# Moving operands read word by word from two places in turn

## The chip, the core and the metric

The kernel runs on one core of one Trainium2 chip. The metric is the device time of one execution, in microseconds; lower is better. Before the change the median of three runs is 2076.68 us (2076.17 to 2077.5). The engines are called by the names in the profile: PE is TensorE's matmuls and PEld its weight loads, DVE is VectorE, ACT ScalarE, POOL GpSimd, SP SyncE.

A matmul holds one operand, the weights or *stationary* operand (128 x 128), in the array. The other, the *moving* operand, is read from the on-chip memory word by word, one column of 128 partitions after the other, and the results go to PSUM in the same order.

## What is computed

One decoder layer on 512 tokens of width 2048, float32: two groups of attention heads side by side, then a gated feed-forward.

```python
def reference(x, attn_norm, w_in, ..., w_out, ffn_norm, w_gate, w_up, w_down):
    h = _rms_norm(x, attn_norm)
    proj = h @ w_in                   # 8 FoX heads (q, k, v, forget gates), 8 NSA heads (q), 2 KV groups x 6, gates
    # FoX: q, k normed per head; softmax(q k' * scale + cum_f[query] - cum_f[key]), causal
    # NSA: compressed keys and values (32-token blocks, stride 16), selected blocks, sliding window,
    #      each a softmax with a distance penalty, added under sigmoid gates
    x = x + concat(o_fox, o_nsa) @ w_out
    h = _rms_norm(x, ffn_norm)
    x = x + (silu(h @ w_gate) * (h @ w_up)) @ w_down     # 5632 wide
    return x
```

## The kernel before

Activations lie transposed: 128 features on the partitions, tokens along the free dimension. Every float32 operand is split into a high part that the matmul's rounded format holds exactly and the low rest, and each product is three matmuls: high x high, high x low, low x high (`mm3`, L258). ScalarE makes the high part and VectorE the low part by subtraction (`split`, L194; `split2`, L208; most of their instructions stand under L92 and L95, the helpers `tt` and `act`).

The stages, in order of time:

- **First loop** (L881): for 16 blocks of input features, load x and four columns of weights, split both, and accumulate the inputs of the compression (`first`, 512 columns, L259 to L261). `scaled` (L389) takes them out of PSUM; for these four results it writes them regrouped for the compression, at a step of 32 words (L394).
- **Projections** (`gemm_steps`, L293; `proj`, L399): 16 heads in 48 matmuls of 512 columns each, with the normalized activations `xg` (in `bigm`) as the moving operand. `values` (L500) makes pairs of value heads the other way round: the activations are stationary, and the weights, 256 columns, move (L540). With `gcols` (the first pair) it also makes the gates. `normed` and `query` turn the results into keys and queries. They run interleaved with the attention heads (`nsa`, L815; `fox`, L839) by hand-written generators (`weave`, `stagger`).
- **Compression** (`compress`, L698): 32 small products per kind, the weights moving.
- **Seven products** (`seven`, L1039): for the last head pairs, a 2 x 2 block product is made with seven products of half size. The forms of the activations (`form`, L1007) move, 256 columns (L1057), and the results are combined from PSUM into two tiles (L1059 to L1079).
- **Output projection**: heads `oT` are split into `om` (`om_parts`, L1201); some column blocks go directly (`two_tiles`, `one_tile`, 512 columns), six by seven products (`one_of_seven`, L1366, 256 columns; sums of heads from `activation_sums`, L1208). `x1_steps` adds the residual, and `raw_forms` (L1242) puts the next stage's inputs, scaled, into four quarters of a raw tile; `form_sums` and `form_parts` make the seven forms from them.
- **Gate and up** (L1763 to L1814): 22 column blocks x gate and up x 4 groups = 176 groups of 42 matmuls with 256 columns (L1792). For each group, SP loads four weight blocks (`fetch`), VectorE makes three sums of them (`sums`), ScalarE the high parts and VectorE the low parts (`part_steps`, L1609), into two slots of `bigm` by turns. A slot can be written again when the matmuls two groups earlier are done. Results of a block are combined on VectorE (`put_together`, `gate_out`, `up_out`) while the next one is computed, in a second set of PSUM banks.
- **Down** (L1888 to L1961): four passes over 22 blocks; each block loads its activations (`load_a`, from DRAM) and weights, splits both (`splits`, L1716), and runs 48 or 36 matmuls of 256 columns (L1931 high weights, L1936 low weights).

From the output projection on, VectorE and ScalarE keep the program's order (`pinned`); in the last two stages the loads do too. All weights are reordered on the host in `kernel`, before the launch.

Of the kernel before, what the change touches and what calls it, by code (L numbers as in the profile page):

```python
# [83 lines left out]
def hybrid_layer(ctx: ExitStack, tc: tile.TileContext, xT, vec, ffb, wfg, wfirst, win, cmpw, wout, wos, wgu, wdn, out):  # L84
# [172 lines left out]

    def mm3(o, lh, ll, rh, rl, start, stop):  # L258
        nc.tensor.matmul(o, lh, rh, start=start, stop=False)  # L259
        nc.tensor.matmul(o, lh, rl, start=False, stop=False)  # L260
        nc.tensor.matmul(o, ll, rh, start=False, stop=stop)  # L261
# [31 lines left out]
    def gemm_steps(o, srcs, mov, name):  # L293

        k = 0
        for j, src in enumerate(srcs):
            wp = load_w(src, f"{name}_{j}")
            for kk in range(src.shape[-1] // P):
                s = slice(kk * P, (kk + 1) * P)
                mm3(o, wp[0][:, s], wp[1][:, s], mov[k][:, 0, :], mov[k][:, 1, :],  # L300
                    k == 0, k == len(mov) - 1)
                k += 1
                yield
# [85 lines left out]
    def scaled(z, name, early=False):  # L389
        t = oxp.tile([P, T], F32, tag="ox", name=f"t_{name}", bufs=OXB) if early else ftile(f"t_{name}")  # L390
        if early:

            b, c = [x.rearrange("p (n l) -> p n l", l=16) for x in (z, rstd)]
            nc.vector.tensor_tensor(t.rearrange("p (l n) -> p n l", l=16), b, c, op=OP.mult)  # L394
        else:
            nc.vector.tensor_tensor(t, z, rstd, op=OP.mult)
# [17 lines left out]
    def squares(name, z):  # L414
# [3 lines left out]
        nc.scalar.activation(sq[half], z[half], AF.Square)  # L418
        nc.scalar.activation(sb[half], z[second_half], AF.Square)
# [34 lines left out]
    def query(name, gain):  # L454
# [3 lines left out]
        split2(r, z, gain)  # L458
        sq = squares(name, z)
# [40 lines left out]
    def values(pair, gcols=None):  # L500
# [10 lines left out]
        for c in range(4):  # L511
# [22 lines left out]
            for b in range(2):  # L534
                for kk in range(4):
                    x = xg[4 * c + kk]
                    for t in range(2):
                        at = slice((2 * b + t) * P, (2 * b + t + 1) * P)
                        for n, xp in enumerate((0, 0, 1)):
                            nc.tensor.matmul(z[2 * b + t][:, :cols[n]], x[:, xp, at], wp[n][kk],  # L540
                                             start=(c == 0 and kk == 0 and n == 0 and (t == 0 or gcols is not None)),
                                             stop=(c == 3 and kk == 3 and n == 2), skip_group_check=True)
# [155 lines left out]
    def compress(which):  # L698
# [3 lines left out]
        for b in range(8):  # L702
# [4 lines left out]
            for jj in range(4):  # L707
                l = 4 * b + jj
                ws = slice(jj * P, (jj + 1) * P)
                nc.tensor.matmul(z, live[which, l // 16][:, l % 16 * P:(l % 16 + 1) * P], wp[:, :, ws],  # L710
                                 start=(l == 0), stop=(l == 31))
# [169 lines left out]
    for k in range(NK):  # L881
# [15 lines left out]
        if k == 0:  # L897
            for wi, xi in ((0, 0), (1, 0), (0, 1)):
                for j in range(4):
                    nc.tensor.matmul(first[j], wp[:, wi, j * P:(j + 1) * P], t[:, xi], start=(wi + xi == 0), stop=False)  # L900
        else:
            for j in range(4):
                c = slice(j * P, (j + 1) * P)
                mm3(first[j], wp[:, 0, c], wp[:, 1, c], t[:, 0], t[:, 1], False, k == NK - 1)
# [134 lines left out]
    def seven(key, names):  # L1039
# [5 lines left out]
        for step, (to, f) in enumerate(products(n)):  # L1045
# [8 lines left out]
            for m, (wp, u, xp) in enumerate(todo):  # L1054
                if m and m % 6 == 0:
                    yield
                nc.tensor.matmul(z, w[wp][:, u * P:(u + 1) * P], form(f, u)[xp], start=(fresh and m == 0),  # L1057
                                 stop=(m == len(todo) - 1), skip_group_check=True)
            if f == 0:  # L1059
                nc.scalar.activation(t0[:, upper], z, AF.Copy)  # L1060
            elif f == 5:
                nc.vector.tensor_tensor(t1[:, lower], z, t0[:, upper], op=OP.add)
            elif f == 4:
                nc.vector.tensor_tensor(t1[:, upper], z, t1[:, upper if n else lower], op=OP.subtract)
            elif f == 1:
                nc.vector.tensor_tensor(t0[:, lower], z, rstd[:, lower], op=OP.mult)
            elif f == 3 and to == 1:
                nc.vector.tensor_tensor(t1[:, upper], z, t0[:, upper], op=OP.add)
            elif f == 6:
                nc.vector.tensor_tensor(t1[:, lower], z, t1[:, lower], op=OP.subtract)  # L1070
            elif f == 2:
                nc.vector.tensor_tensor(t0[:, upper], z, t0[:, upper], op=OP.add)
            else:
                nc.vector.tensor_tensor(t1[:, upper], t1[:, upper], z, op=OP.subtract)
                nc.vector.tensor_tensor(t0[:, upper], z, t0[:, upper], op=OP.add)
# [125 lines left out]
    def om_parts(i):  # L1201
        split(om[i], oT[order[i]])
# [5 lines left out]
    def activation_sums():  # L1208

        last = None  # L1210
        for u in range(HALF):
# [6 lines left out]
            for i in range(2):  # L1218
# [6 lines left out]
                dst = [osums_a[:, u, p, 2 * i:2 * i + 2] for p in range(2)]  # L1225
                act(dst[0], f[i], AF.Copy)
                if last:
                    tt(last[0][1], last[1], last[0][0].bitcast(F32), op=OP.subtract)
                last = dst, f[i]
# [817 lines left out]
```

## Time and profile before

| what | us |
|---|---|
| median of three runs | 2076.68 |
| profiled execution, span | 2076.6 |
| PE busy | 2058.7 |
| PEld busy | 1974.0 |
| DVE busy | 1802.1 |
| ACT busy | 1070.6 |
| POOL busy | 322.5 |
| gate and up, first matmul to first of down (812.14 to 1652.65) | 840.5 |

The profiled execution takes as long as the runs do. "Busy" is the time in which at least one instruction of the engine ran. Matmuls overlap one another in the pipeline, so a busy TensorE says only that there was always a matmul in flight; how fast they follow each other is the time of a stretch over the number that ran in it. Rows of groups have the form: line, engine, operation, output tile <- input tiles, shapes, count | busy us, mean ns of one | idle time before them and what ended it.

### The profile page before, as it was taken

Reading aid. Unit: us, or ns where it says so; the run is one execution under the profiler, and the core shown is the slowest. Engines: PE = TensorE matmul, PEld = TensorE weight load, DVE = VectorE, ACT = ScalarE, POOL = GpSimd, SP = SyncE. Lnnn points to the kernel's source line nnn. Section 1 sums busy time; section 2 is a strip of 40 time slices with the busy share of each in tenths; the row PEclk is TensorE's granted clock in tenths of the full one; section 3 lists DMA queues with packets and bytes.
Section 4 is the critical chain, followed back from the end, with each engine's and each line's share of the span. In section 5 each row is a group of like instructions: output and inputs, shape, how many; then the busy total and the mean of one; then the engine's idle time right before and its main releaser. Section 6 shows DMA issues by size and latency. Waiting matters only on the chain.

```text
span 2076.6 us, 40008 instructions
## 1 busy us (share of the span) xinstructions
PE 2058.7 (99%) x16189; PEld 1974.0 (95%) x16189; DVE 1802.1 (87%) x2744; ACT 1070.6 (52%) x1408; POOL 322.5 (16%) x489
## 2 busy tenths in 40 slices
PE   9999999999999999999999999999999999999999
PEld 7878988899998988999999999999999999999999
DVE  6678779887787877999999999999999987889998
ACT  6555555567675555443343434433433455565554
POOL 1032232422121011111111111111111000000010
PEclk9999999999999999999999999999999999999999
DMA  5685776967785675667767777777777897579865
GB/s 207 205 184 163 179 177 175 221 188 203 223 208 174 203 231 183 176 197 183 201 186 197 195 182 204 190 184 200 186 190 199 254 325 251 153 240 331 295 179 149
DMA packets 142153, 424.22 MB, mean 204 GB/s; under 512 B 17608, under 2 KB 17608, under 8 KB 141968
## 3 DMA queue, kind: packets, MB, share of 16 engines
q1 hardware_dynamic: 91168, 289.21, 41.4%
q0 software_dynamic: 44176, 106.19, 26.7%
q10 hardware_dynamic: 6624, 26.27, 3.3%
q8 instruction: 126, 2.06, 0.4%
q14 instruction: 59, 0.48, 0.1%
HBM read 389.34 MB, written 124.53 MB: 247 GB/s over the span
## 4 chain that ended last, share of the span: by engine, by line
PE 82%; issue 8%; DVE 6%; ACT 2%; POOL 2%; DMA 1%; POOLq 0%; ACTq 0%; SPq 0%; DVEq 0%
PE q L1792 40%; PE pd L1931 13%; PE pd L1936 7%; PE ps_vs L540 2%; PE po L1381 2%; PE ps_vf L540 2%; PE ps_qn L259 1%; PE ps_qn L261 1%; PE ps_qn L260 1%; PE ps_first L261 1%; POOL osum L141 1%; PE ps_first L259 1%; PE po L261 1%; PE po L259 1%; PE po L260 1%
## 5 line engine op out<-in xcount | busy, mean ns | idle before, releaser
L95 ACT ACTIVATE bigm<-r 128x1792 fp32r<-128x1792 f32 x174 | 298.3, 1714 | 467.1 <-PE q L1792 290.9
L92 DVE TENSOR_TENSOR bigm<-r,bigm 128x1792 fp32r<-128x1792 f32 x174 | 351.5, 2020 | 13.2 <-ACT bigm L95 12.5
L92 DVE TENSOR_TENSOR r<-r 128x512 f32<-128x512 f32 x522 | 267.2, 512 | 26.1 <-DMA r<-wgu 13.9
L141 POOL DMA_DIRECT2D wsum<-wdn x176 | 120.3, 690 | 702.3 <-ACT bigm L95 609.6
L1792 PE MATMUL q<-bigm 128*128 128x256 f32 x1848 | 217.4, 276 | 0.5 <-ACT bigm L95 0.3
L1792 PE MATMUL q<-formy,bigm 128*128 128x256 f32 x1848 | 217.0, 276 | 0.0
L1792 PE MATMUL q<-forma,bigm 128*128 128x256 f32 x1848 | 216.8, 276 | 0.0
L1792 PE MATMUL q<-formx,bigm 128*128 128x256 f32 x1848 | 216.8, 276 | 0.0
L1792 PEld LDWEIGHTS q<-bigm 128*128 128x128 f32 x1848 | 213.2, 188 | 0.9 <-ACT bigm L95 0.5
L1792 PEld LDWEIGHTS q<-formy,bigm 128*128 128x128 f32 x1848 | 212.9, 188 | 0.2
L1792 PEld LDWEIGHTS q<-forma,bigm 128*128 128x128 f32 x1848 | 213.0, 188 | 0.1
L1792 PEld LDWEIGHTS q<-formx,bigm 128*128 128x128 f32 x1848 | 212.9, 188 | 0.0
L1931 PE MATMUL pd<-bigm 128*128 128x256 f32 x1200 | 146.9, 276 | 0.0
L1931 PEld LDWEIGHTS pd<-bigm 128*128 128x128 f32 x1200 | 141.0, 188 | 0.0
L92 DVE TENSOR_TENSOR bigm<-wd,bigm 128x1024 fp32r<-128x1024 f32 (+1 forms) x62 | 107.8, 1739 | 12.4 <-ACT bigm L95 12.2
L95 ACT ACTIVATE bigm<-rawm 128x768 fp32r<-128x768 f32 (+2 forms) x72 | 66.0, 927 | 97.8 <-PE pd L1936 63.2
L95 ACT ACTIVATE bigm<-wd 128x1024 fp32r<-128x1024 f32 (+1 forms) x62 | 91.1, 1470 | 10.7 <-DVE wd L92 6.1
L92 DVE TENSOR_TENSOR bigm<-rawm,bigm 128x768 fp32r<-128x768 f32 (+2 forms) x72 | 75.6, 1059 | 23.2 <-ACT bigm L95 22.6
L1936 PE MATMUL pd<-bigm 128*128 128x256 f32 x600 | 80.7, 276 | 0.0
L141 POOL DMA_DIRECT2D fsump<-win x72 | 48.6, 743 | 204.2 <-ACT wp_qn L95 47.6
L1057 PE MATMUL ps_kf<-bigm,wp_kf 128*128 128x256 f32 x576 | 76.1, 281 | 0.7 <-ACT wp_kf L95 0.4
L1936 PEld LDWEIGHTS pd<-bigm 128*128 128x128 f32 x600 | 74.3, 188 | 0.0
(592 smaller groups left out, 4336.2 us busy)
## 6 DMA issues: line engine op xcount, KB each, us to landing
r<-wgu SPq DMA_DIRECT2D x174, 512.0 KB, 4.5
wsum<-wdn POOLq DMA_DIRECT2D x176, 256.0 KB, 5.1
rawm<-ad SPq DMA_DIRECT2D x44, 512.0 KB, 6.9
wd<-wdn SPq DMA_DIRECT2D x40, 512.0 KB, 6.1
wd<-wsum SPq DMA_DIRECT2D x40, 512.0 KB, 7.1
ad<-cb ACTq DMA_DIRECT2D x22, 896.0 KB, 6.6
fsump<-win POOLq DMA_DIRECT2D x72, 256.0 KB, 6.0
rawm<-ad SPq DMA_DIRECT2D x44, 384.0 KB, 3.5
```

Of the source, the lines that this page charges most:

```text
L92: return pin(nc.vector.tensor_tensor(*args, op=op))
L95: return pin(nc.scalar.activation(*args, **kw))
L141: d = nc.gpsimd.dma_start(step[0], step[1], **step[2])
L259: nc.tensor.matmul(o, lh, rh, start=start, stop=False)
L260: nc.tensor.matmul(o, lh, rl, start=False, stop=False)
L261: nc.tensor.matmul(o, ll, rh, start=False, stop=stop)
L540: nc.tensor.matmul(z[2 * b + t][:, :cols[n]], x[:, xp, at], wp[n][kk], start=(c == 0 and kk == 0 and n == 0 and (t == 0 or gcols is not No ...
L1057: nc.tensor.matmul(z, w[wp][:, u * P:(u + 1) * P], form(f, u)[xp], start=(fresh and m == 0), stop=(m == len(todo) - 1), skip_group_check=True)
L1381: nc.tensor.matmul(q[b][:, h * 256:(h + 1) * 256], w[wp][:, u * P:(u + 1) * P], a[xp], start=(h == 0 and u == 0 and wp == 0 and xp == 0), ...
L1792: nc.tensor.matmul(o, w[wp][:, fb, cs], a[:, xp, fa], start=(k == 0 and h == 0 and wp == 0 and xp == 0), stop=(g == NG - 1 and kk == 1 and ...
L1931: nc.tensor.matmul(b[q][k][:, h * 256:(h + 1) * 256], w[0][:, fb, q * P:(q + 1) * P], a[xp][:, fa], start=(j == 0 and h == 0 and xp == 0), ...
L1936: nc.tensor.matmul(b[q][k][:, h * 256:(h + 1) * 256], w[1][:, fb, q * P:(q + 1) * P], a[0][:, fa], start=False, stop=(j == NJ - 1), skip_g ...
```

## The change

Four views of a row of words are added. In the names below n is the row's length, cut into j equal pieces, and each piece into two halves.

- `_in_turn`: read word 0 of the first half, word 0 of the second, word 1 of the first, and so on.
- `_like`: the same shape over words as they lie (the output of a matmul that reads `_in_turn`).
- `_mixed`: every second word, first the even ones, then the odd ones.
- `_apart`: the two halves, one after the other; the same shape as `_mixed`.

```python
def mm(o, w, x, j=1, **kw):
    nc.tensor.matmul(_like(o, j), w, _in_turn(x, j), **kw)

def mm3t(o, lh, ll, rh, rl, start, stop, j=1):
    mm(o, lh, rh, j, start=start, stop=False)
    mm(o, lh, rl, j, start=False, stop=False)
    mm(o, ll, rh, j, start=False, stop=stop)

def _in_turn(x, j=1): return x.rearrange("p (j b a) -> p j a b", j=j, b=2)
def _like(x, j=1):    return x.rearrange("p (j a b) -> p j a b", j=j, b=2)
def _mixed(x, j=1):   return x.rearrange("p (j a b) -> p j b a", j=j, b=2)
def _apart(x, j=1):   return x.rearrange("p (j b a) -> p j b a", j=j, b=2)
```

The matmuls of `gemm_steps`, the first loop, `values` without `gcols`, `compress`, `seven`, the output projection, gate and up, and down use them; those of the attention, of the transposes and of `values` with `gcols` stay as they were. PSUM is written in order. So that results mean the same tokens, either the operand is written in a changed order or the result is read in one:

- Projections, first loop, `seven`: the activations lie as before, so the results lie mixed in PSUM. What takes them out reads `_mixed` and writes `_apart`:

```diff
-            nc.vector.tensor_tensor(t, z, rstd, op=OP.mult)
+            nc.vector.tensor_tensor(_apart(t), _mixed(z), _apart(rstd), op=OP.mult)
...
-        split2(r, z, gain)
-        sq = squares(name, z)
+        split2([_apart(x) for x in r], _mixed(z), gain)
+        sq = squares(name, z, _mixed)
...
-                nc.vector.tensor_tensor(t1[:, lower], z, t0[:, upper], op=OP.add)
+                nc.vector.tensor_tensor(l1, z, u0, op=OP.add)
```

  with `z = _mixed(z)` and `l0, u0, l1, u1` the `_apart` views of the two halves of `t0` and `t1`. The regrouping of the four first results (L394) reads a step of two as well.
- Output projection, gate and up, down: the parts are written `_apart` from a `_mixed` read, and the results lie in order:

```diff
-        split(om[i], oT[order[i]])
+        split2([_apart(om[i][:, p], 2) for p in range(2)], _mixed(oT[order[i]], 2))
...
-        act(raw[:, 1:3] if second else raw[:, 0:8:7], t.rearrange("p (h t) -> p h t", h=2), AF.Copy, scale=v1(V_FN + n))
+        for h, f in enumerate((1, 2) if second else (0, 7)):
+            act(_apart(raw[:, f]), _mixed(t[:, h * 256:(h + 1) * 256]), AF.Copy, scale=v1(V_FN + n))
...
-            split2(a, rawa.pop(i))
+            split2([_apart(x, n) for x in a], _mixed(rawa.pop(i), n))
```

  In `activation_sums` the same is done for the sums of heads.
- `values` and `compress`, where weights move: the host writes them in the changed order (`_unmix`, for the value pairs after the first and for `cmpw`).

The matmul of gate and up, as an example of all:

```diff
-                                nc.tensor.matmul(o, w[wp][:, fb, cs], a[:, xp, fa],
-                                                 start=(k == 0 and h == 0 and wp == 0 and xp == 0),
-                                                 stop=(g == NG - 1 and kk == 1 and wp == 1), skip_group_check=True)
+                                mm(o, w[wp][:, fb, cs], a[:, xp, fa],
+                                   start=(k == 0 and h == 0 and wp == 0 and xp == 0),
+                                   stop=(g == NG - 1 and kk == 1 and wp == 1), skip_group_check=True)
```

More of the change, by code (lines that the diff above doesn't have):

```diff
@@ L412, in hybrid_layer, with squares @@
     second_half = slice(P // 2, P)
-    def squares(name, z):
+    def squares(name, z, laid=_apart):
         sq = ftile(f"sq_{name}")
         sb = ap_.tile([P, T], F32, tag="sb", name=f"sb_{name}")
-        nc.scalar.activation(sq[half], z[half], AF.Square)
-        nc.scalar.activation(sb[half], z[second_half], AF.Square)
+        nc.scalar.activation(_apart(sq[half]), laid(z[half]), AF.Square)
+        nc.scalar.activation(_apart(sb[half]), laid(z[second_half]), AF.Square)
         nc.vector.tensor_tensor(sq[half], sq[half], sb[half], op=OP.add)
@@ L539, in values @@
                         for n, xp in enumerate((0, 0, 1)):
-                            nc.tensor.matmul(z[2 * b + t][:, :cols[n]], x[:, xp, at], wp[n][kk],
-                                             start=(c == 0 and kk == 0 and n == 0 and (t == 0 or gcols is not None)),
-                                             stop=(c == 3 and kk == 3 and n == 2), skip_group_check=True)
+                            (nc.tensor.matmul if gcols is not None else mm)(
+                                z[2 * b + t][:, :cols[n]], x[:, xp, at], wp[n][kk],
+                                start=(c == 0 and kk == 0 and n == 0 and (t == 0 or gcols is not None)),
+                                stop=(c == 3 and kk == 3 and n == 2), skip_group_check=True)
                     yield
@@ L709, in compress @@
                 ws = slice(jj * P, (jj + 1) * P)
-                nc.tensor.matmul(z, live[which, l // 16][:, l % 16 * P:(l % 16 + 1) * P], wp[:, :, ws],
-                                 start=(l == 0), stop=(l == 31))
+                nc.tensor.matmul(z.rearrange("p s (a b) -> p s a b", b=2), live[which, l // 16][:, l % 16 * P:(l % 16 + 1) * P],
+                                 wp[:, :, ws].rearrange("p s (b a) -> p s a b", b=2), start=(l == 0), stop=(l == 31))
                 if l % 2:
@@ L899, in hybrid_layer @@
                 for j in range(4):
-                    nc.tensor.matmul(first[j], wp[:, wi, j * P:(j + 1) * P], t[:, xi], start=(wi + xi == 0), stop=False)
+                    mm(first[j], wp[:, wi, j * P:(j + 1) * P], t[:, xi], start=(wi + xi == 0), stop=False)
         else:
@@ L1224, in activation_sums @@
                     tt(f[1][:, 1], f[1][:, 0], b[:, 0], op=OP.add)
-                dst = [osums_a[:, u, p, 2 * i:2 * i + 2] for p in range(2)]
-                act(dst[0], f[i], AF.Copy)
+                dst = [_apart(osums_a[:, u, p, 2 * i:2 * i + 2].rearrange("p f t -> p (f t)"), 2) for p in range(2)]
+                src = _mixed(f[i].rearrange("p f t -> p (f t)"), 2)
+                act(dst[0], src, AF.Copy)
                 if last:
                     tt(last[0][1], last[1], last[0][0].bitcast(F32), op=OP.subtract)
-                last = dst, f[i]
+                last = dst, src
                 yield
@@ L1380, in one_of_seven @@
                 for xp in range(2 - wp):
-                    nc.tensor.matmul(q[b][:, h * 256:(h + 1) * 256], w[wp][:, u * P:(u + 1) * P], a[xp],
-                                     start=(h == 0 and u == 0 and wp == 0 and xp == 0),
-                                     stop=(u == HALF - 1 and wp == 1), skip_group_check=True)
+                    mm(q[b][:, h * 256:(h + 1) * 256], w[wp][:, u * P:(u + 1) * P], a[xp],
+                       start=(h == 0 and u == 0 and wp == 0 and xp == 0),
+                       stop=(u == HALF - 1 and wp == 1), skip_group_check=True)
     loads, front, behind = {}, {}, {}
@@ L1742, in splits @@
         if i == 4 * NJ - 1:
-            split2(a, rawa.pop(i))
+            split2([_apart(x, n) for x in a], _mixed(rawa.pop(i), n))
         return [[x.rearrange("p (f c) -> p f c", f=n) for x in y] for y in (w, a)]
@@ L1930, in block @@
                                 for xp in range(2):
-                                    nc.tensor.matmul(b[q][k][:, h * 256:(h + 1) * 256], w[0][:, fb, q * P:(q + 1) * P], a[xp][:, fa],
-                                                     start=(j == 0 and h == 0 and xp == 0), stop=False, skip_group_check=True)
+                                    mm(b[q][k][:, h * 256:(h + 1) * 256], w[0][:, fb, q * P:(q + 1) * P], a[xp][:, fa],
+                                       start=(j == 0 and h == 0 and xp == 0), stop=False, skip_group_check=True)
                     for q in qs:
@@ L2030 @@
         "win": win,
-        "cmpw": np.concatenate(cw, axis=0),
+        "cmpw": _unmix(np.concatenate(cw, axis=0), P, np),
         "wout": _tiles(wo, np),
```

54 lines of the change are left out of this document (34 added, 20 removed).

## Prediction

> **What bounds the kernel now.** I read the page's first two parts and its shares of the chain that ended last, then the table by stretches, then single stretches of TensorE's timeline, and last who waits for whom.
>
> ```profile
> span 2076.6 us, 40008 instructions
> PE 2058.7 (99%) x16189; PEld 1974.0 (95%) x16189; DVE 1802.1 (87%) x2744; ACT 1070.6 (52%) x1408; POOL 322.5 (16%) x489
> ...
> PEclk9999999999999999999999999999999999999999
> ...
> PE 82%; issue 8%; DVE 6%; ACT 2%; POOL 2%; DMA 1%; POOLq 0%; ACTq 0%; SPq 0%; DVEq 0%
> ```
>
> TensorE is busy 99% of the span at its full granted clock and is 82% of the chain. So the question is whether its matmuls stream as fast as they could. The table by stretches (gate and up; down; output projection; everything from the first projections to the last heads) gives their pace:
>
> ```profile
> core 0: us, PE busy (x) PEld busy (x) DVE busy (x) ACT busy (x) POOL busy (x), PEclk, DMA share, GB/s
> 860.00:1640.00 780.00, 780.00 (x6882) 780.00 (x6881) 740.02 (x991) 313.93 (x225) 113.81 (x166) 1.00 0.74 193
> 1660.00:2060.00 400.00, 400.00 (x3528) 400.00 (x3527) 346.98 (x360) 228.11 (x230) 15.10 (x23) 1.00 0.76 246
> 670.00:810.00 140.00, 138.61 (x858) 123.65 (x857) 110.94 (x154) 75.78 (x90) 15.90 (x29) 1.00 0.63 207
> 100.00:670.00 570.00, 559.62 (x3709) 504.18 (x3708) 457.04 (x1013) 356.55 (x724) 159.59 (x235) 1.00 0.73 192
> ```
>
> In gate and up one matmul of 256 columns takes 780.00/6882 = 113.3 ns, in down 400.00/3528 = 113.4 ns, with no gap anywhere. The timeline of a stretch of the output projection has the 512-column ones; between the two rows lie 24 others:
>
> ```profile
> 654.26 0.40 PE L260 MATMUL po<-bigm,wp_o 128*128 128x512 f32 x1
> ...
> 659.94 0.39 PE L261 MATMUL po<-bigm,wp_o 128*128 128x512 f32 x1
> ```
>
> That is (659.94 - 654.26)/25 = 227.2 ns. The two widths fit one line through nothing: 113.3/256 = 0.443 ns a column, 227.2/512 = 0.444. There is no fixed cost per matmul in it, but a cost per word read. A matmul with few columns is bounded by its weight load instead; the timeline and the by-line view of the transposes:
>
> ```profile
> 249.80 0.60 PE L633 MATMUL pT_s<-ident,p_s 128*128 128x128 f32 x4
> L633 PE MATMUL pT_s<-ident,p_s x80: 270/272/329, 148.2 to 371.7; 128*128 128x128 f32 x80
> ```
>
> Four in 600 ns of which the last takes its whole 272: (600 - 272)/3 = 109 ns each, with 128 columns and a weight load each. So a new 128x128 weight every 109 ns is possible, and 113.3 ns for 256 columns isn't the weight load. It is the moving operand. As an estimate from these rows, a column could take 109/256 = 0.426 ns at most, if its word came in time; 0.443 is taken.
>
> The Trainium skill (TensorE: Matmul & The Clock Gate, Back-to-back issue gap) puts a warm matmul at N/2.4 + 2.5 ns, which is 109.2 and 215.8 ns here; the trace disagrees by 4.1 and 11.4 ns.
>
> Does the place of a read matter? In gate and up, group 55 of 176 has its low weight part 8 words further on (L1613, i % 48 == 7). Three rows of the timeline, one group each:
>
> ```profile
> 1071.62 4.92 PE L1792 MATMUL q<-formy,bigm 128*128 128x256 f32 x42
> 1076.38 5.02 PE L1792 MATMUL q<-bigm 128*128 128x256 f32 x42
> 1081.24 4.93 PE L1792 MATMUL q<-forma,bigm 128*128 128x256 f32 x42
> ```
>
> From its start to the next one's the first group takes 4.76 us, the second 4.86. The second differs in that shift (and in which form it reads), and 0.10 us over its 14 matmuls with low parts is 7 ns each. So the pace hangs on where words are read, and a new order of reading can move it.
>
> **The change part by part.** (1) **The matmuls.** The same instructions, columns and PSUM places; only the moving words come alternately from two places, 128 words apart (256 in the projections with 512 columns). Its count, by line (L1792, L1931, L1936, L1057, L1381 in this order, busy of each over the whole span):
>
> ```profile
> 0.00:2077.00 2077.00, 839.90 (x7392) 839.22 (x7392) 1.00 0.72 204
> 0.00:2077.00 2077.00, 297.37 (x2464) 287.58 (x2464) 1.00 0.72 204
> 0.00:2077.00 2077.00, 158.12 (x1232) 148.30 (x1232) 1.00 0.72 204
> 0.00:2077.00 2077.00, 169.86 (x1344) 162.55 (x1344) 1.00 0.72 204
> 0.00:2077.00 2077.00, 58.32 (x504) 57.91 (x504) 1.00 0.72 204
> ```
>
> and, from the by-line view, the value projections that change, and the first and last of the seven 512-column groups on L260:
>
> ```profile
> L540 PE MATMUL ps_vf<-wp_vf,bigm 128*128 128x256 f32 x384 | 53.0, 283 | 0.2 <-ACT sb_qf L419 0.2
> L540 PE MATMUL ps_vs<-wp_vs,bigm 128*128 128x256 f32 x192 | 27.5, 284 | 0.0
> ...
> L260 PE MATMUL po<-bigm,wp_o 128*128 128x512 f32 x160 | 62.5, 391 | 0.0
> ...
> L260 PE MATMUL ps_ks<-bigm,wp_ks 128*128 128x512 f32 x32 | 12.5, 391 | 0.0
> ```
>
> Gate and up have 7392, down 2464 + 1232 = 3696, the rest 1344 + 504 + 384 + 192 = 2424 and 64 of compression, so 2488. Of 512 columns there are 480 in the output projection (L259, L260, L261, 160 each), 768 in 16 plain projections of 48, and 192 in the first loop: 1440.
>
> No row shows a matmul whose moving words alternate. The near end is the weight load, 109 ns; the far one is a second step for each word (rival D). I take the near one: the loss is a small share of each word's time and depends on places, as a read that must fetch ahead would lose, and two places in turn give each of them twice the time. That is a reading of the rows and not shown by them. At 109 ns a 256-column matmul gains 4.3 ns; a 512-column one, at 216, gains 11.
>
> (2) **Gate and up** don't get it all, for VectorE is nearly full there. Who VectorE waits for, in 860 to 1640 us:
>
> ```profile
> DVE r L92 <- DMA r<-wgu: 12.3, 18, 2.5
> DVE bigm L92 <- ACT bigm L95: 11.1, 36, 0.6
> ```
>
> ScalarE's wait goes with a faster TensorE, since ScalarE itself waits for matmuls to free the weight slots. Without any wait VectorE needs 780 - 23.4 = 756.6 us, 97.0%, or 109.9 ns a matmul; with the DMA's 12.3 us it needs 768.9, or 111.7. So VectorE, not TensorE, ends this stage between 7392 x 3.4 = 25 and 7392 x 1.6 = 12 us sooner. I take 19.
>
> (3) **Down.** VectorE waits there, 1660 us to the end, mostly for ScalarE:
>
> ```profile
> DVE bigm L92 <- ACT bigm L95: 34.8, 50, 2.1
> DVE formx L92 <- ACT formx L95: 14.2, 23, 0.9
> ```
>
> 49 us in about 410 is room for the 3696 x 4.3 = 16 us that TensorE saves. I take 16.
>
> (4) **The rest**: 1440 x 11 = 16 and 2488 x 4.3 = 11, together 27 us. In 100:670 VectorE is busy 457.04 of 570.00 and TensorE 559.62, so most is on TensorE; a quarter I give back to heads and weight parts that become late, as 8% of the chain is issue and 6% VectorE. I take 20.
>
> (5) **New orders on VectorE and ScalarE.** Results and parts are now read at a step of two words: projection results, the parts of heads for the output projection, and the 88 activation splits of down. The trace has no step of two, but it has contiguous reads, and one operation (L394) that writes at a step of 32 words:
>
> ```profile
> L394 DVE TENSOR_TENSOR t_kc<-ps_first,rstd x2: 1114/1126/1139, 55.2 to 56.2; 128x512 f32<-128x512 f32 x2
> ...
> L396 DVE TENSOR_TENSOR t_qn<-ps_qn,rstd x8: 680/692/693, 120.0 to 327.8; 128x512 f32<-128x512 f32 x8
> ```
>
> So a step costs from 0 to (1126 - 692)/512 = 0.85 ns a word. In down, with 1024 or 768 words a split, that is up to 0.76 us, 88 times, 67 us, over a room of 49 - 16 = 33 us: 34 us late at worst. I take 0, because two words is nearer to contiguous than 32 is, and the waits just shown cover a little more than nothing.
>
> (6) **One ScalarE copy becomes two** in the raw forms, 16 times. Rows by form, 512 words and 256:
>
> ```profile
> L95 ACT ACTIVATE raw<-x1r,vt 128x512 f32<-128x512 f32 x14 | 9.5, 712 | 2.0 <-DMA x1r<-x1d 2.0
> L95 ACT ACTIVATE vf<-ps_vf,rcol 128x256 fp32r<-128x256 f32 x8 | 3.8, 470 | 2.9 <-PE ps_vf L540 2.3 <-DVE vf L215 0.6
> ```
>
> 2 x 470 - 712 = 228 ns, 3.6 us in all. In 670:810 ScalarE is busy 75.78 of 140, which hides it; uncovered it costs these 3.6 us. No DMA, wait or buffer is added, and the host's reordering of weights isn't timed.
>
> **Sum:** 19 + 16 + 20 = 55 us off the profiled span of 2076.6 us, which is the median of the runs (2076.68) as well: 2022 us.
>
> **The rivals.** **B, order doesn't matter.** The lost time could belong to a count of words and not to their places. For it speaks how exactly 113.3 and 227.2 stand to each other; against it the slower group 55. It gives 2077, within 0.2% (4 us, about what a measurement of this kernel can tell from no change).
>
> **C, TensorE gains only part.** Group 55 shows that 8 words between a weight and its moving words cost 7 ns; two places meet the weights in another way, and half of the gain may go: 27 us off, 2049. VectorE's end in gate and up (12 us only) works the same way.
>
> **D, slower: every word comes from a new place.** If a read keeps only the last few neighbouring words at hand, each word of two places in turn is fetched anew. For it speaks L394, where far steps make VectorE take 1126 instead of 692 ns. It decides as soon as the mean word costs more than today's 0.443 ns. At a second step for each word, twice 0.426, 256 columns take 218 ns: 13576 x 100 + 1440 x 200 ns (100 ns a 256-column matmul, as a round figure) = 1650 us, some 3720 us. Against it: nothing of TensorE's, whose rows show no strided moving operand at all.
>
> The Trainium skill (Advanced Engine Details and Errata, SBUF Cachelines) states this rule: lines of 16 bytes, at least two hits on a line needed to hide the latency, and a penalty when each access meets a different line. By that rule D would come true; no run here shows it for TensorE.
>
> **E, strided splits end down**: (5)'s 34 us late against a gain of 55, so 2056.
>
> **How the numbers follow.** Forecast (2022, with its bounds 1996 to 2035): 0.56. Its low end is all of TensorE's gain: 7392 x 4.3 + 16 + 27 = 75 us, or 2002, and a little more if the weight load can go under 109. C: 0.15, E: 0.06, B: 0.09, D: 0.14. Faster by over 0.2% are the forecast, C and E, 0.77; within 0.2% is B, 0.09; slower is D, 0.14. The range reaches over C, E and B: 1996 to 2080. It leaves out D, and little else.
>
> **What would show it.** Right: 7392 matmuls of L1792 at 109.9 to 111.7 ns, with TensorE's first waits for VectorE in that stage; down at about 109 ns with VectorE's waits for ScalarE cut to about 33 us; the 512-column stretch at about 216 ns; strided VectorE rows of 512 words still near 690 ns. Wrong: 113.3 ns as before (B), 218 ns (D), splits of down well over their times of before (E). The forecast falls with the one thing that no row shows, the price of a word when two places take turns.

## The result, and the profile after

The changed kernel takes 2046.13 us (median of 4 runs, 2045.45 to 2048.68) against 2077.09 us of before on the same chip (4 runs, 2076.17 to 2078.1): a ratio of 0.9851, with a 95% interval from 0.9837 to 0.9865. That is 31 us less; 55 were forecast. The profiled execution has a span of 2044.6 us. The first part of its page and the shares of its chain:

```profile
span 2044.6 us, 40066 instructions
...
PE 2015.6 (99%) x16189; PEld 1946.2 (95%) x16189; DVE 1809.7 (89%) x2744; ACT 1109.1 (54%) x1424; POOL 323.4 (16%) x489
...
PEclk9999999999999999999999999999999999999999
...
PE 60%; DVE 2%; ACT 1%; issue 1%; DMA 0%; ACTq 0%; DVEq 0%
```

TensorE is busy as fully as before, at the same clock, with the same 16189 matmuls: they follow each other faster. The table by stretches (gate and up; down; columns as in the prediction's table):

```profile
840.00:1620.00 780.00, 780.00 (x6985) 779.84 (x6985) 747.74 (x1001) 322.38 (x230) 114.82 (x168) 1.00 0.72 196
1640.00:2040.00 400.00, 400.00 (x3583) 399.96 (x3582) 360.38 (x373) 250.92 (x229) 15.08 (x23) 1.00 0.74 245
```

One matmul of 256 columns takes 780.00/6985 = 111.7 ns in gate and up and 400.00/3583 = 111.6 in down, where 113.3 and 113.4 stood before. In the output projection a run of matmuls of 512 columns without a gap, by line (count: shortest/median/longest, first and last start):

```profile
L259 PE MATMUL po<-bigm,wp_o x144: 378/379/379, 641.6 to 672.4; 128*128 128x512 f32 x144
```

From the first start to the last lie 143 matmuls, (672.4 - 641.6)/143 = 215.4 ns; with the starts taken to the nanosecond it is 215.8. It was 227.2 in the prediction's stretch, and 226.7 over the 141 matmuls of the same kind from 654.0 to 685.8 us there. All matmuls of the changed kind now stand under L259, the line of `mm`.

By stage, from the starts of the first matmul of each output tile (po, q, pd) to the next one's, in us:

| stage | before | after | gain | forecast |
|---|---|---|---|---|
| start to output projection | 634.0 | 620.8 | 13.2 | 20 for both |
| output projection | 178.2 | 177.6 | 0.6 | |
| gate and up | 840.5 | 828.8 | 11.7 | 19 |
| down, to the end | 423.9 | 417.4 | 6.5 | 16 |
| span | 2076.6 | 2044.6 | 32.0 | 55 |

So gate and up, down and the stages ahead gained, and each fell short of its forecast; the 0.6 us of the output projection are no gain that can be told from none, for other profiles of the same code there show 178.1 and 178.5 us (`after_again` and `late_undone`, below). Three questions are left: what ends a 256-column matmul at 111.67 and not at 109 ns; what the order of reading does; and where the output projection's gain went.

### The profile page after: what moved, and what is told of

The parts are those of the page before. It is cut to its first block, busy times and chain, and to the rows that moved or that the text cites. A ratio compares the mean times of both kernels' runs of the same rounds, so it can differ in the third digit from the quotient of the medians.

```text
span 2044.6 us, 40066 instructions
## 1 busy us (share of the span) xinstructions
PE 2015.6 (99%) x16189; PEld 1946.2 (95%) x16189; DVE 1809.7 (89%) x2744; ACT 1109.1 (54%) x1424; POOL 323.4 (16%) x489
## 4 chain that ended last, share of the span: by engine, by line
PE 60%; DVE 2%; ACT 1%; issue 1%; DMA 0%; ACTq 0%; DVEq 0%
PE q L259 40%; PE pd L259 20%; PE po L259 0%; DVE bigm L92 0%; DVE t L92 0%; DVE raw L92 0%; ACT raw L95 0%; DVE wp_o L92 0%; ACT bigm L95 0%; DVE ca L92 0%; ACT wp_o L95 0%; DVE r L92 0%; DMA x1r<-x1d 0%; DVE cb L92 0%; DVE formy L92 0%
## 5 line engine op out<-in xcount | busy, mean ns | idle before, releaser
L259 PE MATMUL q<-bigm 128*128 128x256 f32 x1848 | 213.9, 275 | 0.6 <-ACT bigm L95 0.4
L259 PE MATMUL q<-formy,bigm 128*128 128x256 f32 x1848 | 213.9, 275 | 0.5 <-ACT bigm L95 0.5
L259 PE MATMUL q<-formx,bigm 128*128 128x256 f32 x1848 | 213.7, 275 | 0.3 <-ACT bigm L95 0.3
L259 PE MATMUL q<-forma,bigm 128*128 128x256 f32 x1848 | 213.8, 275 | 0.0
L259 PEld LDWEIGHTS q<-bigm 128*128 128x128 f32 x1848 | 210.0, 192 | 1.0 <-ACT bigm L95 0.6
L259 PEld LDWEIGHTS q<-formy,bigm 128*128 128x128 f32 x1848 | 210.0, 192 | 0.9 <-ACT bigm L95 0.7
L259 PE MATMUL pd<-bigm 128*128 128x256 f32 x1800 | 210.3, 275 | 0.0
L259 PEld LDWEIGHTS q<-formx,bigm 128*128 128x128 f32 x1848 | 209.9, 192 | 0.4 <-ACT bigm L95 0.4
L259 PEld LDWEIGHTS q<-forma,bigm 128*128 128x128 f32 x1848 | 210.0, 192 | 0.2 <-DVE bigm L92 0.2
L259 PEld LDWEIGHTS pd<-bigm 128*128 128x128 f32 x1800 | 206.3, 192 | 0.0
L259 PE MATMUL po<-bigm,wp_o 128*128 128x512 f32 (+1 forms) x696 | 132.7, 349 | 5.6 <-DVE wp_o L92 3.2
L259 PEld LDWEIGHTS po<-bigm,wp_o 128*128 128x128 f32 x696 | 114.1, 190 | 20.3 <-DVE wp_o L92 5.2
L95 ACT ACTIVATE bigm<-rawm 128x768 fp32r<-128x768 f32 (+2 forms) x72 | 83.0, 1165 | 77.6 <-PE pd L259 53.2
L259 PE MATMUL pd<-formx,bigm 128*128 128x256 f32 x888 | 102.6, 275 | 0.0
L259 PEld LDWEIGHTS pd<-formx,bigm 128*128 128x128 f32 x888 | 100.8, 192 | 0.0
L259 PE MATMUL ps_qn<-bigm,wp_qn 128*128 128x512 f32 x384 | 100.1, 387 | 0.7 <-DVE wp_qn L92 0.7
```

The lines of the kernel that those rows point to most:

```text
L95: return pin(nc.scalar.activation(*args, **kw))
L259: nc.tensor.matmul(_like(o, j), w, _in_turn(x, j), **kw)
```

## Experiments

### What sets 111.67 ns: the weight load

Theory 1: a new weight every 111.67 ns is TensorE's limit in a long run, whatever moves. Theory 2: the moving operand, though read from two places in turn, still takes longer than the 109 ns of a weight load. `p_weights` changes the four passes of down: the weights are read at steps of 2, 1, 2 and 4 words, and in the second and third pass each matmul becomes two of 128 columns with the moving words in order, so that the moving words are half as many and can't be what bounds them. Its result is another; it is run for the times alone.

```diff
-                                    mm(b[q][k][:, h * 256:(h + 1) * 256], w[0][:, fb, q * P:(q + 1) * P], a[xp][:, fa],
-                                       start=(j == 0 and h == 0 and xp == 0), stop=False, skip_group_check=True)
+                                    probe(ps_, b[q][k][:, h * 256:(h + 1) * 256], stepped(ps_, w[0], fb, q), a[xp][:, fa],
+                                          start=(j == 0 and h == 0 and xp == 0), stop=False)
...
+    def stepped(n, w, fb, q):
+        f = w.rearrange("p f c -> p (f c)")
+        step = (2, 1, 2, 4)[n]
+        at = min(fb * T + q * P, f.shape[-1] - step * P)
+        return f[:, at:at + step * P:step]
```

> Only down differs from the changed kernel, and its result is another: the weights are read at other places (pass 1 and 3 of 4 counted from 1: at a step of two words; pass 4: at a step of four), and in passes 2 and 3 each matmul of 256 columns is made in two of 128, moving words in order, each with its own weight load. Theory T1, the 111.7 ns of a 256-column matmul are the pace of the weight loads: pass 2 takes 111.7 ns for each 128-column matmul, though its moving words need at most 57. Rival T2, the moving words still lose time in two places and weights could go on at the 109 ns of the transposes: pass 2 takes 109. If weights lose time by being read in order, as moving words did, passes 1, 3 and 4 differ from 111.7 in either direction; if not, pass 1, 3 and 4 stay at 111.7.

The one execution took 2373.24 us. One stretch of each pass in the table by stretches (us, PE, PEld, DVE, ACT, POOL, clock, DMA share, GB/s):

```profile
1640.00:1740.00 100.00, 100.00 (x847) 100.00 (x846) 79.92 (x57) 59.98 (x38) 0.00 (x0) 1.00 0.82 286
1760.00:1920.00 160.00, 160.00 (x1435) 160.00 (x1435) 64.42 (x78) 47.84 (x59) 0.00 (x0) 1.00 0.33 100
1940.00:2160.00 220.00, 220.00 (x1870) 220.00 (x1869) 94.80 (x87) 57.75 (x41) 8.15 (x15) 1.00 0.45 147
2200.00:2360.00 160.00, 160.00 (x683) 160.00 (x682) 72.19 (x95) 42.25 (x52) 5.12 (x6) 1.00 0.30 80
```

The second row decides it. With 128 columns in order a matmul takes 160.00/1435 = 111.5 ns, and over the 1584 starts of that pass 111.64: the pace of the 256-column ones of the change. Half the moving words cost as much time, so it isn't the moving operand. Weights at a step of 2 take 118 ns, whether 256 words move in turn (first row, 118.1) or 128 in order (third, 117.6), and at a step of 4 the load takes 234 ns (fourth). The second pass alone couldn't tell the weight load from some other cost that each matmul has once; that the pace moves with the step of the weights in the other passes is what points to the load. So theory 2 falls, and theory 1 fits all four passes: at 256 columns the change took the moving operand below the weight load, and all that was left to gain was 113.4 - 111.67 = 1.7 ns. In the second stretch VectorE is busy 64.42 of 160.00, so it isn't VectorE either.

### What the order does: ten orders of reading

`p_orders` and `p_orders2` give the direct column blocks of the output projection, one after the other, different orders of reading their 512 moving words (the results then stand in another order), and the first loop one more. The instruction and its count stay; 512 columns are far enough above the weight load to show the moving operand.

```diff
+    def pattern(n, x):
+        if n == 0:
+            return x
+        if n == 1:
+            return x.rearrange("p (b a) -> p a b", b=4)
+        if n == 5:
+            return x.rearrange("p (a b) -> p b a", b=2)
+        if n == 6:
+            return x.rearrange("p (b a) -> p a b", b=16)
+        if n == 7:
+            return x.rearrange("p (b a c) -> p a b c", b=2, c=2)
+        return x.rearrange("p (a b c) -> p a c b", b=2, c=4)
```

> Orders of reading for 512-column matmuls, where a weight load (112 ns) is hidden. The tokens of the output projection and of the compression come out in another order. By block: 0 and 8 in order; 1 and 9 four places in turn; 5 and 13 every second word, then the others; 6 and 14 sixteen places 32 words apart; 7 and 15 two words from each of two places; first loop: two places 4 words apart. Theory F, a read loses time when the next word is its neighbour's neighbour in the same small stretch of memory and none when consecutive words lie far apart: 216 ns for four, sixteen and 4-apart places, 227 in order, between for pairs and every second word. Rival L, a read needs two words from the same 16-byte line: far more than 216 for sixteen and four places, 227 or less only for pairs, every second word and in order.

One execution took 2101.09 us. Its rows by line, in the order of n above (0, 1, 5, 6, 7):

```profile
L286 PE MATMUL po<-bigm,wp_o x48: 387/389/398, 647.3 to 658.0; 128*128 128x512 f32 x48
...
L288 PE MATMUL po<-bigm,wp_o x72: 436/451/451, 658.2 to 678.3; 128*128 128x512 f32 x72
...
L290 PE MATMUL po<-bigm,wp_o x96: 615/631/651, 738.0 to 781.1; 128*128 128x512 f32 x96
...
L292 PE MATMUL po<-bigm,wp_o x96: 612/627/627, 781.5 to 822.9; 128*128 128x512 f32 x96
...
L294 PE MATMUL po<-bigm,wp_o x96: 505/506/525, 823.3 to 854.5; 128*128 128x512 f32 x96
```

From first to last start, over the count less one: in order (658.0 - 647.3)/47 = 228 ns, four places in turn 283, every second word and then the others 453.5, sixteen places 435, two words from each of two places 328.5 (starts taken to the nanosecond). So a word can cost twice the 0.443 ns of a read in order, as rival D feared, 453.5/512 = 0.886, if not in the order that was chosen. The first loop's order in that run, two places 4 words apart, took 216.

Theory for the second run: the words of even and of odd number in the sequence run in two streams, each at half the pace, and a stream loses when its next word lies in another group of four words. In order, a stream changes group at every second word of its own; with two places in turn, at every fourth. The second run takes orders that tell this from "neighbours in memory are cheap" (`p_orders2`, in the same places of the code):

```diff
+        if n == 0:
+            return x.rearrange("p (b a) -> p a b", b=2)
+        if n == 1:
+            return x.rearrange("p (a b c) -> p a c b", b=2, c=2)
+        if n == 5:
+            return x.rearrange("p (b a s) -> p s a b", b=2, s=2)
+        if n == 6:
+            return x.rearrange("p (b a s) -> p s a b", b=2, s=4)
+        if n == 7:
+            return x.rearrange("p (b a) -> p a b", b=8)
+        return x.rearrange("p (a b c) -> p a c b", b=2, c=8)
```

> More orders for 512-column matmuls in the same places as before; tokens of the output projection and the compression come out in another order. Blocks 0 and 8 two places in turn; 1 and 9 words 0, 2, 1, 3 of every four; 5 and 13 two places in turn, in each every second word first; 6 and 14 two places in turn, in each every fourth word first; 7 and 15 eight places in turn; first loop two places 8 words apart. Theory C, the words are fetched over two channels, the even ones of the sequence and the odd ones, and each channel loses time when its next word lies in another group of four words: in order a channel takes 2 words of a group (227 ns), two places give 4 (216), every second word or sixteen places 1 (452, 435). Then: 227 for 0 2 1 3 and for every second word of two places, about 440 for every fourth word of two places, 216 for 8 apart. Rival F2, only the distance of neighbours in the sequence counts (near 3 words or more is free, next word costs): 216 for all with two places, also where each is read at a step of two or four. Eight places: over the 283 of four, by C at most 440.

One execution took 2093.41 us. The rows by line, again in the order 0, 1, 5, 6, 7:

```profile
L286 PE MATMUL po<-bigm,wp_o x48: 378/379/379, 650.4 to 660.5; 128*128 128x512 f32 x48
...
L288 PE MATMUL po<-bigm,wp_o x72: 387/389/399, 660.8 to 676.9; 128*128 128x512 f32 x72
...
L290 PE MATMUL po<-bigm,wp_o x96: 387/389/398, 735.7 to 757.4; 128*128 128x512 f32 x96
...
L292 PE MATMUL po<-bigm,wp_o x96: 615/630/637, 757.6 to 800.6; 128*128 128x512 f32 x96
...
L294 PE MATMUL po<-bigm,wp_o x96: 667/667/741, 801.1 to 847.4; 128*128 128x512 f32 x96
```

All orders together, by how many words of a stream lie in one group before it changes (ns per matmul of 512 columns, from the starts):

| words before a stream changes group | order | ns |
|---|---|---|
| 4 | two places in turn, 256, 128, 8 or 4 words apart | 216 |
| 2 | in order | 227 |
| 2 | words 0, 2, 1, 3 of each four | 227 |
| 2 | two places, first the even words of each | 227.5 |
| 1 | four places 128 apart | 283 |
| 1 | two words from each of two places | 328.5 |
| 1 | sixteen places 32 apart | 435 |
| 1 | every second word, then the others | 453 |
| 1 | two places, every fourth word of each | 453 |
| 1 | eight places 64 apart | 488 |

The three levels are as the theory has them: the order 0, 2, 1, 3 never leaves its four words and still takes 227, and two places read by even words take 227 and not 453. What the theory doesn't give are the differences in the last level, 283 to 488; it expected one value there, and at most 440 for eight places, which took 488. So the two streams sort the orders that were run into levels, and the mechanism behind them is not shown and stays open. Each order stands for the blocks of one execution; in the stretches shown the matmuls follow each other at an even pace.

### Gains add up by stage

`late_undone` undoes the order in gate and up and in down alone (the matmuls, the splits of down and the two raw copies).

```diff
-                                mm(o, w[wp][:, fb, cs], a[:, xp, fa],
+                                nc.tensor.matmul(o, w[wp][:, fb, cs], a[:, xp, fa],
...
-            split2([_apart(x, n) for x in a], _mixed(rawa.pop(i), n))
+            split2(a, rawa.pop(i))
```

> Gate, up and down read in order again, everything before as in the changed kernel. Theory that the stages' gains are the matmuls' alone and add up: 11.7 + 6.5 = 18 us back, 2064 us; gate and up 113.3 ns a matmul. Rival, that faster projections only move the wait to the later stages or that the two-step copies in down cost something: 2060 or less.

2065.91 us (2064.1 to 2066.45), a ratio to before of 0.9943 (0.9926 to 0.9959). In the table by stretches its last two stages are those of before, to one matmul in the count:

```profile
840.00:1620.00 780.00, 780.00 (x6882) 780.00 (x6881) 739.14 (x989) 315.19 (x226) 114.56 (x168) 1.00 0.73 192
1660.00:2060.00 400.00, 400.00 (x3529) 400.00 (x3528) 346.38 (x369) 221.38 (x225) 15.06 (x23) 1.00 0.74 240
```

Gate and up took 840.2 us and down 423.9, the earlier stages 622.0 and 178.5. So these two stages gave back (840.2 - 828.8) + (423.9 - 417.4) = 17.9 us, as the theory says, and nothing that was late in an earlier stage moved into them. The whole run gave back 2 us more; they lie in the stages before, whose matmuls are the same as after the change and which take 620.0 to 622.2 us up to the output projection in the profiles that have them.

### Where the output projection's gain went

Its 480 matmuls of 512 columns and 504 of 256 should have brought 480 x 11 + 504 x 1.7 = 6.1 us; the stage became 0.6 shorter, so 5.5 are missing. TensorE's waits in that stage, before and then after (engine, what waits <- what ended it: us in all, times, longest):

```profile
PE po L259 <- DVE t_vf L1070: 1.0, 1, 1.0
PE s_f L259 <- DVE st_f L602: 1.0, 1, 1.0
PE po L1381 <- ACT wp_o L95: 0.6, 1, 0.6
PE po L261 <- DVE wp_o L92: 0.5, 1, 0.5
```

```profile
PE po L259 <- DVE wp_o L92: 3.2, 4, 1.4
PE po L259 <- ACT wp_o L95: 1.3, 2, 1.1
PE po L259 <- DVE t_vf L1082: 1.2, 1, 1.2
```

TensorE waits 4.5 us for weight parts (wp_o) where it waited 1.1: 3.4 of the missing 5.5 us. All its idle time in the stage went from 3.3 us (174.76 busy of 178.10) to 8.2 (169.36 of 177.60), 4.9 more. A faster matmul asks sooner for the next part, and VectorE or ScalarE isn't there yet. Three theories of why were tried.

The first: reading at a step of two makes VectorE and ScalarE late. `psum_order` writes the parts and forms in plain order again, and reads the results `_mixed` from PSUM instead, in the output projection, in gate and up and in down.

```diff
-        split2([_apart(om[i][:, p], 2) for p in range(2)], _mixed(oT[order[i]], 2))
+        split(om[i], oT[order[i]])
...
-            split2([_apart(x, n) for x in a], _mixed(rawa.pop(i), n))
+            split2(a, rawa.pop(i))
...
-        tt(t62, b[0], rstd, op=OP.mult)
+        tt(_apart(t62, 2), _mixed(b[0], 2), _apart(rstd, 2), op=OP.mult)
```

> Same matmuls as the changed kernel, but from the output projection on the parts are copied in order and the results, which then lie mixed in PSUM, are read at a step of two words there. Theory: only on-chip reads outside PSUM at a step of two cost VectorE and ScalarE time (rows of 686 to 782 and 621 to 774 ns), and that is what the output projection gave back (its stage went from 178.2 to 177.6 us where its matmuls gain about 6): stage near 172 us, gate and up and down unchanged at 111.7 ns a matmul, run 5 us faster than the changed kernel (about 2041). Rival: the stage is held by loads and by ScalarE's order, not by the copies: 177 us and no gain.

2043.68 us (2043.22 to 2044.2), ratio 0.9839 (0.9824 to 0.9853), and 2043.9 us (2042.91 to 2045.04), ratio 0.9835 (0.9822 to 0.9849), in the second run below. The output projection took 176.9 us, 0.7 less than after. The steps aren't what makes the parts late.

The second: the combining work on VectorE that is queued ahead of the next weight parts. `low_first` is `psum_order` with the weight parts of the next piece always first; `after_again`, the changed kernel once more, ran beside it.

```diff
-            n = 1
+            n = 0
```

> As psum_order (2043.7), but in the output projection a piece's low weight parts stand on VectorE ahead of the forms' sums of the next stage, not behind them. Theory, what the output projection gave back is this order on VectorE: TensorE's waits for wp_o there (4.8 us in the changed kernel, 4.4 in psum_order) fall to about 2 and the run takes 2 to 3 us less, 2041. Rival, the slots of the weight parts and the loads hold it, so the wait only moves to ScalarE or to the next piece: 2043 to 2045.

> The changed kernel once more beside low_first on one chip: 2046, steady gate and up at 111.7 ns a matmul.

`low_first` took 2052.77 us (2049.95 to 2054.58; ratio 0.9887, 0.9871 to 0.9904) and `after_again` 2048.68 (2046.69 to 2049.92; ratio 0.9864, 0.9849 to 0.9879). The output projection became 182.7 us, 5.8 longer than in `psum_order`; in `after_again`, on the same chip, it was 178.1. In `low_first` VectorE waits longer for ScalarE, and so then does TensorE:

```profile
DVE wp_o L92 <- ACT wp_o L95: 38.7, 29, 4.0
```

```profile
PE po L259 <- ACT wp_o L95: 4.6, 6, 1.2
```

The same row of VectorE was 22.1 us in `psum_order`. An earlier place in the queue makes VectorE stand still until ScalarE has made the high part. The theory falls: TensorE waits 5.7 us for weight parts (4.6 for ScalarE's, 1.1 for VectorE's) where about 2 were expected.

The third: reloads of the residual's rows (x1r) land late, and ScalarE, standing at the copies that read them, makes the next weight part late. In `psum_order` it waited 5.0 us for them, against 2.0 before the change. `x1r_early` ties the reload to one weight part sooner, `x1r_free` to none; `psum_again` is `psum_order` beside them.

```diff
-                tc.add_manual_dep(d.ins, highs[-1].ins.name, PACE)
+                tc.add_manual_dep(d.ins, highs[-2].ins.name, PACE)
```

```diff
-            if pair:
+            if False:
```

> The same kernel as psum_order, on the chip of the next two, to compare them with: 2041 to 2050 us, output projection 176.9 us (2042.4 us span there). In that stage TensorE's idle time ended by weight parts was 2.8 us (VectorE) and 1.6 us (ScalarE), ScalarE's by the loads x1r 5.0 us (before the change 2.0).

> psum_order with the reloads of the residual's rows (x1r, L1300) released one high weight part sooner. Theory: with the faster matmuls these loads land after ScalarE reaches the copies that read them (ScalarE waits 5.0 us for them, against 2.0 before the change); the weight parts queued behind those copies are late, and TensorE waits. Then ScalarE's waits for x1r go to about 1 us, and the output projection is 2 to 4 us shorter than in psum_again (173 to 175 us). Rival: the weight parts are late because the two slots of a weight part come free too late for the faster matmuls, whatever is queued; then the stage changes by less than 1 us, though ScalarE's waits for x1r go.

> psum_order with the reloads x1r released as soon as their tile is free, with no wait for a high weight part. Theory (late reloads): as in x1r_early or a little more, output projection 173 to 175 us. Rival (weight slots): less than 1 us off psum_again, or some us longer if the early reloads crowd out the weight loads ws_o, for which ScalarE waited 5.0 us in psum_order.

| kernel | us (range) | ratio (95%) | output projection | ScalarE for x1r | TensorE for wp_o |
|---|---|---|---|---|---|
| psum_again | 2043.9 (2042.91 to 2045.04) | 0.9835 (0.9822 to 0.9849) | 176.5 | 5.2 | 4.1 |
| x1r_early | 2043.36 (2042.43 to 2044.46) | 0.9832 (0.9818 to 0.9845) | 177.4 | none | 3.8 |
| x1r_free | 2042.18 (2041.01 to 2043.6) | 0.9827 (0.9814 to 0.9841) | 174.3 | 0.3 | 2.3 |

The waits of TensorE behind the last column, of `x1r_early` and then of `x1r_free`:

```profile
PE po L259 <- DVE wp_o L92: 2.0, 2, 1.6
PE po L259 <- ACT wp_o L95: 1.8, 3, 0.8
```

```profile
PE po L259 <- DVE wp_o L92: 1.5, 3, 0.5
...
PE po L259 <- ACT wp_o L95: 0.8, 1, 0.8
```

This one is split. In `x1r_early` ScalarE's waits for x1r are gone and the stage is no shorter, as the rival said. In `x1r_free` the stage is 2.2 us shorter, and TensorE's waits for weight parts are 1.8 us less. So reloads that are merely no longer late don't help; free ones do a little, and why is open. The changed kernel itself says the same. In its output projection ScalarE hardly waits for x1r at all:

```profile
ACT raw L95 <- DMA x1r<-x1d: 0.9, 1, 0.9
```

and the stage takes 177.6 us, against 176.9 in `psum_order` with its 5.0 us of such waits, and 178.5 in `late_undone` with 5.4. Late reloads are not where the gain went. What is shown is that most of it went into waits for weight parts; why the parts come late is not shown. That the two slots of weight parts are the cause, the rival, was not tried. `x1r_free` has the lowest median of all kernels run, but its range and its interval overlap those of `psum_again`.

## The prediction, step by step

The 2046 us lie in the stated range, but that range reached over the rivals C, E and B. The forecast's own bounds were 1996 to 2035, and the time lies outside them. The direction was right, and so was the reading that the moving words set the pace and that their order moves it, with the price at 512 columns. The reason given for it, a read that fetches ahead and has twice the time in two places, is not shown by any run. Of 55 us 32 came in the profile; gate and up lack 7, down 9.5 and the rest 6, and most of that comes from one term, the price of a 256-column matmul.

**Step 1, the price of a matmul.** For 512 columns 216 ns was right (215.8). For 256 columns the near end, 109 ns from the transposes, was wrong, and this is the term that was mis-sized: the weight load of a long run takes 111.6 to 111.7 ns, as the second pass of `p_weights` (111.64) and gate and up (111.67) show. A 256-column matmul gains 1.7 ns, not 4.3. The transposes come in fours; why their loads follow at 109 ns stays open. The Trainium skill (TensorE: Matmul & The Clock Gate, Back-to-back issue gap) gives, as the isolated gap of a warm matmul, 512/2.4 + 2.5 = 215.8 ns, and the trace after the change agrees to the tenth; for 256 columns its formula gives 109.2, and the trace disagrees by 2.5 ns, because here the load of the weights comes last. That 109.2 and the transposes' 109 agree is no support for the price: neither was a long run of weight loads.

**Step 2, gate and up.** The forecast had VectorE end the stage at 109.9 to 111.7 ns. The number 111.7 came out, for another reason. VectorE's waits in 840 to 1620 us, after:

```profile
DVE r L92 <- DMA r<-wgu: 12.8, 14, 2.0
DVE bigm L92 <- ACT bigm L95: 2.5, 9, 0.9
```

ScalarE's part fell from 11.1 to 2.5, as said. But TensorE doesn't wait for VectorE in that stretch: of the 6982 steps from one of its starts to the next, all but two are 111 or 112 ns, and down runs at the same pace with VectorE idle for 40 of 400 us. So it is a coincidence that the number lay at the edge of the forecast: VectorE's bound and the weight load were within 0.1 ns of each other, and the total couldn't tell which was met. The even steps and `p_weights` do. At 7392 x 1.7 = 12.6 us the term would have been right; 11.7 was measured.

**Step 3, down.** 3696 x 1.7 = 6.3 us, measured 6.5, in place of 16. The same term. VectorE's waits for ScalarE fell from 49 us to 27.6 + 9.5 = 37; about 33 were forecast.

**Step 4, the rest.** 1440 x 11 = 16 stands; 2488 x 4.3 becomes 2488 x 1.7 = 4, together 20. Of this 13.8 came. The quarter given back to heads and late weight parts was the right idea and a little too small: 6 of 20 us, nearly all in the output projection.

**Step 5, strided reads.** From the on-chip memory they are not free, but hidden. By-form rows of down's splits, after:

```profile
L95 ACT ACTIVATE bigm<-rawm 128x1024 fp32r<-128x1024 f32 x29 | 40.3, 1391 | 45.5 <-PE pd L259 44.0 <-issue 1.4
L92 DVE TENSOR_TENSOR bigm<-rawm,bigm 128x1024 fp32r<-128x1024 f32 x29 | 39.3, 1354 | 7.3 <-ACT bigm L95 7.2
```

and the same in the kernel before:

```profile
L92 DVE TENSOR_TENSOR bigm<-rawm,bigm 128x1024 fp32r<-128x1024 f32 x29 | 35.4, 1222 | 8.9 <-ACT bigm L95 8.5
...
L95 ACT ACTIVATE bigm<-rawm 128x1024 fp32r<-128x1024 f32 x29 | 30.8, 1062 | 57.2 <-PE pd L1936 55.4 <-issue 1.8
```

A step of two makes ScalarE's copy of 1024 words 1391 - 1062 = 329 ns longer, 0.32 ns a word, and VectorE's subtraction 132 ns, 0.13 a word: inside the bounds of 0 to 0.85. The sign that strided VectorE rows of 512 words stay near 690 ns failed for reads from the on-chip memory; the split of the heads, before and then after:

```profile
L92 DVE TENSOR_TENSOR bigm<-o,bigm 128x512 fp32r<-128x512 f32 x16 | 10.5, 686 | 0.0
```

```profile
L92 DVE TENSOR_TENSOR bigm<-o,bigm 128x512 fp32r<-128x512 f32 x16 | 11.8, 782 | 0.2 <-ACT bigm L95 0.2
```

That is 0.19 ns a word. Down lost nothing by the longer splits: it takes 417.4 us with them and 417.3 in `psum_order`, which has none. From PSUM the step costs VectorE nothing; the projections' row, 692 ns before, after the change:

```profile
L405 DVE TENSOR_TENSOR t_qn<-ps_qn,rstd x8: 682/692/692, 116.0 to 317.7; 128x512 f32<-128x512 f32 x8
```

**Step 6, two copies for one.** 28 copies of 622 ns for 14 of 712 are 7.4 us more on ScalarE, twice the 3.6 of the forecast, which took 470 ns from a copy that reads in order; these read at a step. `psum_order` has one copy again and reads no on-chip memory at a step in that stage, and the stage changed by 0.7 us: hidden, nearly.

**The rivals.** B (order doesn't matter) fell with the 512-column pace. C came nearest in time, 2049, but not by its mechanism: no half of the loss is left at 512 columns, and the distance to the weights no longer shows. From 860 to 1640 us of the kernel before, all 51 steps between starts that are over 115 ns lie at the low weight parts of groups 55, 103 and 151, the ones with the shift, most of them 120 ns; group 59 and others that read the same form run at 113.33. So the shift made group 55 slow, and not the form. After the change every group from the tenth on runs at 111.67, these three too, with the same shift. D is wrong for this order and right for others: every second word takes 453 ns, 2.1 times 216. The Trainium skill's rule (Advanced Engine Details and Errata, SBUF Cachelines: lines of 16 bytes, two hits on a line hide the latency) doesn't fit these rows: two places in turn meet another line at each word and run fastest, and every second word has two hits on each line and takes twice as long. E did not happen, as step 5 shows for down.

## What to carry to other kernels

When a matmul's pace fits one line through nothing over its columns, the time goes with the words that move and not with the instruction, and another order of reading them is worth a trial; the fit alone doesn't say that it will help. But first look for the limit that lies just below, here the weight load of a long run, and take its price from a run as long, not from a burst of four. Wide matmuls gain all (11 ns at 512 columns), narrow ones what is left above the weight load (1.7 ns at 256). Where results or operands must be reordered for it, VectorE can do it while it reads PSUM, which cost nothing here; reading the on-chip memory at a step costs VectorE and ScalarE time, which here was hidden: `psum_order`, which avoids it in the later stages, ran at a ratio of 0.9839 against 0.9851, with intervals that overlap.

## What the runs showed of the hardware

- Reading the moving operand in plain order isn't the fastest order: 227 ns for 512 words, against 216 from two places in turn. Six of the ten orders are far slower, 283 to 488 ns, and "every second word", which looks harmless, takes 453. All this is for float32 words.
- A new float32 weight per matmul comes every 111.6 ns in a long run, every 118 with its words at a step of two and every 234 at a step of four.
- A step of two costs ScalarE 0.32 ns a word (1024 words) and VectorE 0.13 to 0.19 (1024 and 512 words) when read from the on-chip memory, and VectorE nothing when read from PSUM (512 words, 692 ns both ways).
